# A hybrid trunk in fp32: merge products spread behind their copies, cross-attention K and V between them, output projection in two halves, convolution taps loaded instead of built

## The chip, the cores and the metric

One core of a Trainium2 chip runs the whole kernel in one launch. The core has five engines that run their own instruction queues in order: TensorE (PE, with PEld for its weight loads), VectorE (DVE), ScalarE (ACT), GpSimd (POOL) and SyncE (SP), which here issues nearly all DMA transfers. The metric is the device time of one execution in microseconds (us), lower being better.

## The reference

Two layers over 512 positions of width 1024, all in fp32. Layer 0 mixes tokens with a gated DeltaNet, layer 1 with a Conformer convolution module; after the mixer each layer cross-attends into a fixed memory of 256 rows and applies a squared-ReLU MLP.

```python
def step(state, inp):                      # per chunk of 64 positions, per head
    qd, kd, uc, wc, ai, gl = inp
    v_new = uc - einsum("bhck,bhkv->bhcv", wc, state)
    o = einsum("bhck,bhkv->bhcv", qd, state) + einsum("bhcj,bhjv->bhcv", ai, v_new)
    state = state * exp(gl)[..., None, None] + einsum("bhck,bhcv->bhkv", kd, v_new)
    return state, o
# uc, wc: solution of (I + lower) sol = [v*beta, k*beta*exp(g)], a triangular solve per chunk

def conformer_conv(h, ...):
    u = h @ w_pw1 + b_pw1
    u = u[..., :D] * sigmoid(u[..., D:])
    c = causal_depthwise_conv(u, w_dw) + b_dw          # width 31, per channel
    c = silu(layer_norm(c, ln_g, ln_b))
    return c @ w_pw2 + b_pw2

for layer in range(2):
    h = h + mixer(rms_norm(h))                          # DeltaNet ends in  o @ w_out
    h = h + memory_cross_attention(rms_norm(h), rms_norm(mem), w_q, w_kv, w_o)
    h = h + square(relu(rms_norm(h) @ w_up)) @ w_down
return rms_norm(h, final_norm)
```

## The kernel before

Activations are kept transposed, as eight tiles of 128 channels by 512 positions. An fp32 product is made of three matmuls on values that are split into a high and a low part (`mm3`): high by high, high by low, low by high. Weights come in halves of 128x1024 (512 KB, tile `raw`, three buffers), each loaded by SP, cast to its high part by ScalarE (`wh`, L214) and subtracted by VectorE to give its low part (`wl`, L72). Three split halves may stand ready (`NW`, `NRAW`).

The DeltaNet section is written as a list of units of TensorE work (`mains`). Units 0 to 65 are the projections of k, q, z and v, for head group 0 (heads 0 to 3) and then for group 1: a head's projection is two units of 12 matmuls, so are the z units. Units 66 to 81 are K and V of the first cross-attention, which need only the memory. Beside the units, side work is put at (unit, rank) by `S.at`, and `run` (L275) emits a unit and then its side work by rank. The tile framework turns this into one fixed queue per engine when the kernel is built, with an order that its own planning may change slightly; on the chip each engine works through its queue in order.

The side work that matters here, for each group of four heads:

- `conv_head` (L441 on): the short convolution. For a V head all three further taps are made as a ScalarE scaling (`cvq`, L452) and a POOL add (`cva`, L72); a SiLU on ScalarE (L459) follows a unit later.
- `fs_steps`: a forward substitution on VectorE that inverts 32x32 diagonal blocks (tiles `fst` and `X`), in the units from 20 and from 50 (`FS`). `fs_end` transposes the result (`TB`, `UB`).
- `mg_a` copies the inverse into place for a head: four copies to `x0` on ScalarE (L570), four to `u0` on POOL (L571). It stands at unit 32 (group 0) and 61 to 63 (group 1), `MG`.
- `mg_w`, `mg_y`, `mg_y`, `mg_end`: the merge of the blocks, matmuls of width 96 and less (L579, L591), with a ScalarE copy (`w`, L581; `y`, L594) after each. They stand one to four units behind `mg_a`.
- `v2` transposes V (`vt`, L616), `rec` is the recurrence over four chunks in three steps each, from unit 39 and unit 68 (`REC`), and `o_gate`, `o_norm`, `head_out` finish the heads.

The memory is loaded at unit 53 (`MEM`), squared (`msq`, ScalarE and POOL adds), summed by matmul (`mssq`, L752), scaled by POOL (`mem`, L72) and multiplied by its gain (`mh`, L774). `mem_gain` stands at units 62 and 63, `MGAIN` before the K units. After `run` the output projection w_out is made with all eight heads per output tile (`proj` on `os_`, L1247 on), and `do_ev` adds the residual x, which is loaded again by SP at unit 74.

In the conformer the first three of eight channel blocks are convolved by VectorE (`ca`, L75), paced by `taps_dve`, the other five by TensorE, with a position-phased layout (`xg`, sixteen small DMAs per block, L1014) and nine tap matrices of 128x512 per block. POOL builds the tap matrices from the parameters and an identity (`taps`, L971). In this stretch K of the second cross-attention is computed too.

A line of the changed kernel is two to four lower than the same line here.

Of the kernel before, what the change touches and what calls it, by code (L numbers as in the profile page):

```python
# [9 lines left out]
F32R = mybir.dt.float32r  # L10
# [4 lines left out]
P = 128  # L15
NT = 512
NDVE = 3
# [9 lines left out]
_o += 16  # L27
OFF["w_conv"] = _o
_o += 24 * 4
OFF["w_dw"] = _o  # L30
_o += 8 * 144
OFF["w_tap"] = _o
_o += NDVE * 31
OFF["out_norm"] = _o
# [3 lines left out]


@with_exitstack  # L40
def tile_trunk(ctx, tc, xT, memT, prm_d, adt_d, bdw_d, fin_d, w_ab, w_kq, w_v, w_z, w_dno, w_pw1, w_pw2,
               w_q, w_k, w_vv, w_o, w_up, w_dn, yT):
    nc = tc.nc
    pe, act, dve, pool = nc.tensor, nc.scalar, nc.vector, nc.gpsimd
# [17 lines left out]
    def psum(s="ps"):  # L62
        return psp.tile([P, NT], F32, tag="ps", name=nm(s))
# [4 lines left out]
    def const(shape, s, dt=F32):  # L68
        return cp.tile(list(shape), dt, tag=s, name=s)

    def tt(e, o, a, b, op):
        e.tensor_tensor(out=o, in0=a, in1=b, op=op)  # L72
# [16 lines left out]
    def over_c(t, n=4):  # L89
        return t.unsqueeze(1).to_broadcast([P, n, t.shape[1]])  # L90
# [6 lines left out]
    def load_x():  # L97
        r = []
        for t in range(KT):
            h = slot(s="x")  # L100
            nc.sync.dma_start(out=h, in_=xT[t * P:(t + 1) * P, :])
            r.append(h)
        return r

    nc.sync.dma_start(out=prm[:, 0:NVEC], in_=prm_d[:, 0:NVEC])
    wab = const([P, P], "wab")
    nc.sync.dma_start(out=wab, in_=w_ab)
    raw0 = wp.tile([P, 1024], F32, tag="raw", name="raw0", bufs=NRAW)
    nc.sync.dma_start(out=raw0, in_=w_kq[0][:, 0:1024])
# [26 lines left out]
    headx = const([P, 32], "headx")  # L136
    dve.tensor_reduce(out=headx, in_=ident.rearrange("p (x c) -> p x c", c=4), op=ALU.add, axis=AX.X)
    dve.tensor_reduce(out=headm, in_=headx.rearrange("p (a h) -> p h a", h=8), op=ALU.add, axis=AX.X)
    ident4 = const([P, 32], "ident4")
    eps_rms = const([P, 1], "eps_rms")  # L140
    pool.memset(eps_rms, EPS)
    eps_ln = const([P, 1], "eps_ln")
# [75 lines left out]
    def wnext(key, hf):  # L218
        i = ws["next"]
        assert order[i] == (key, hf), (order[i], key, hf)  # L220
        while ws["load"] < min(i + NRAW + 2, len(order)):
            wload()
        while ws["split"] < min(i + (NW if i else 1), len(order)):
            wsplit()
        ws["next"] += 1
        return ws["hl"].pop(i)
# [11 lines left out]
    def proj(w, xs, ps, k0=0, k1=KT):  # L238
        for k in range(k0, k1):
            mm3(ps, wk(w, k), xs[k], k == 0, k == KT - 1)  # L240
# [729 lines left out]

    def taps(m):  # L971

        w = OFF["w_dw"] + 144 * m
        TAPS[m] = []
        for i in range(9):
            t = slot(s="tap")
            tt(pool, t.rearrange("p (a c) -> p a c", c=32), over_c(ident4, 16),
               prm[:, w + 16 * i:w + 16 * i + 16].unsqueeze(2).to_broadcast([P, 16, 32]), ALU.mult)
            TAPS[m].append(t)

    def conformer(norm, hres, nxt):
# [143 lines left out]

    nc.sync.dma_start(out=prm[:, NVEC:NPRM], in_=prm_d[:, NVEC:NPRM])
    nc.sync.dma_start(out=adt, in_=adt_d.partition_broadcast(P))
    for b in range(4):
        bs = slice(32 * b, 32 * b + 32)
        pool.tensor_copy(ident4[bs, :], ident[bs, bs])  # L1130
    abp = const([P, 2 * P], "abp", F32R)
    ab3 = abp.rearrange("p (k x) -> p k x", k=KT)
    act.copy(ab3[:, :, 0:16], wab.rearrange("p (k x) -> p k x", k=KT))
    tt(dve, ab3[:, :, 16:32], wab.rearrange("p (k x) -> p k x", k=KT), ab3[:, :, 0:16].bitcast(F32), ALU.subtract)
# [68 lines left out]
    for gq in range(2):  # L1203
        f0, nf = FS[gq]
        S.at(f0, 5, D.fs_begin, gq)
        for i in range(nf):
            S.at(f0 + i, 6, D.fs_steps, gq, i * 31 // nf, (i + 1) * 31 // nf)
        S.at(f0 + nf, 0, D.fs_end, gq)
        S.at(f0 + 1, 7, D.norm_k, gq)
        for i in range(4):  # L1210
            h = 4 * gq + i
            m = MG[gq] + i * MSTEP[gq] // 2
            S.at(m, 1, D.mg_a, h)
            S.at(f0 + nf - 4 + i, 5, D.mg_pre, h)
            for j, f in enumerate((D.mg_w, D.mg_y, D.mg_y, D.mg_end)):
                S.at(m + 1 + j, 1, f, h)
        for c in range(4):
            S.at(max(at["v", 4 * gq + 3] + V2[gq], f0 + nf), 3, D.v2, gq, c)
        n = 0
        for c in range(4):  # L1220
            for step in range(3):
                S.at(REC[gq] + n, 0, D.rec, gq, c, step)
                n += 1
            S.at(REC[gq] + n, 5, D.o_gate, gq, c)
        S.at(REC[gq] + n + 1, 1, D.o_norm, gq)
# [3 lines left out]
    S.at(MEM + 9, 3, mem_stat)  # L1229
    S.at(at["kv"] - MGAIN, 6, mem_gain, 0, 0)  # L1230
    S.at(at["kv"] - MGAIN + 1, 6, mem_gain, 0, 1)
    os_, xres = [], []
    for i in range(4):
        S.at(HO + i, 6, lambda i=i: os_.append(D.head_out(i)))
    S.at(REC[1] + 6, 8, lambda: xres.extend(load_x()))
    run(mains, S)

    h = []
# [2 lines left out]
    def do_ev(m, ps):  # L1241
        hn = slot(s="h")
        tt(dve, hn, ps, xres[m], ALU.add)
        h.append(hn)
        n1.add(m, hn)

    def do_w(m):  # L1247
        return wnext(("do", m // 2), m % 2), psum("do")

    w0, p0 = do_w(0)  # L1250
    proj(w0, os_, p0, 0, 4)
    w1, p1 = do_w(1)
    proj(w1, os_, p1, 0, 4)
    for i in range(4, 8):
        os_.append(D.head_out(i))
    proj(w0, os_, p0, 4, 8)
    do_ev(0, p0)
    proj(w1, os_, p1, 4, 8)
    do_ev(1, p1)
    for m in range(2, 8):  # L1260
        w, ps = do_w(m)
        proj(w, os_, ps)
        do_ev(m, ps)
    n2 = Norm("mlp_norm0")
    h = xattn(0, n1, h, n2)
    n3 = Norm("cv_norm", deng=pool)
# [50 lines left out]
    mlp(1, n5, h, None, None, finish, load)  # L1317


NSLOT = 66  # L1320
NCV = 6
NRAW = 3
PRE = ((2, 4), (2, 6))
# [11 lines left out]
FS = ((20, 9), (50, 8))  # L1335
MSTEP = (0, -1)
MG = (32, 63)
V2 = (4, 3)
MGAIN = 4
HO = 76  # L1340
REC = (39, 68)
MEM = 53
MLP_ORDER = [("up", 0), ("up", 1), ("dn", 0), ("up", 2), ("dn", 1), ("up", 3), ("dn", 2), ("dn", 3)]
TAP_RATE = 0.75
CONV_SEQ = [("p", i) for i in range(16)] + [("k", i) for i in range(16)]
# [11 lines left out]
def _pack_a(np, w, order=None):  # L1357
    t = _tiles_a(np, w)
    if order is not None:
        t = t[order]  # L1360
    m = t.shape[0]
    return np.ascontiguousarray(t.reshape(m // 2, 2, 128, 1024).transpose(0, 2, 1, 3).reshape(m // 2, 128, 2048))
# [7 lines left out]

def _taps(np, w):

    wt = w.T.reshape(8, 4, 32, 31)
    e = np.zeros((4, 32, 8, 4, 9, 4), w.dtype)
    for s in range(4):
        for u in range(9):
            for r in range(4):
                d = r - s + 4 * u
                if 0 <= d <= 30:
                    e[s, :, :, :, u, r] = wt[:, :, :, 30 - d].transpose(2, 0, 1)  # L1380
    e = e.reshape(128, 8, 4, 9, 4)
    return np.concatenate([e[:, :, :, 0:8].reshape(128, 8, 128), e[:, :, :, 8].reshape(128, 8, 16)],
                          axis=2).reshape(128, 1152)


def _layout(np, i):
    i = {k: np.asarray(v) for k, v in i.items()}
    f = np.ascontiguousarray

    def vec(v):  # L1390
        return v.reshape(-1, 128).T

    r = {}
    r["xT"] = f(i["x"][0].T)
    r["memT"] = f(i["mem"][0].T.reshape(4, 2, 128, 256).transpose(0, 2, 1, 3).reshape(4, 128, 512))
    vecs = [i["dn_norm"][0], i["cv_norm"][0], i["xa_norm"][0], i["xa_norm"][1], i["xa_mem_norm"][0],
            i["xa_mem_norm"][1], i["mlp_norm"][0], i["mlp_norm"][1], i["cv_ln_g"][0],
            i["cv_ln_b"][0], i["cv_b_pw2"][0], i["cv_b_pw1"][0]]
    cols = [vec(v) for v in vecs]
    cols.append(i["dn_w_conv"][0].T.reshape(24, 128, 4).transpose(1, 0, 2).reshape(128, 96))  # L1400
    cols.append(_taps(np, i["cv_w_dw"][0]))
    cols.append(i["cv_w_dw"][0].T.reshape(8, 128, 31)[:NDVE].transpose(1, 0, 2).reshape(128, NDVE * 31))
    cols.append(i["dn_out_norm"][0].reshape(128, 1))
    r["prm"] = f(np.concatenate(cols, axis=1))
    r["adt"] = f(np.concatenate([i["dn_a_log"][0], i["dn_dt_bias"][0]]))
    r["bdw"] = f(i["cv_b_dw"][0])
    r["fin"] = f(i["final_norm"])
    w = i["dn_w_in"][0]
    r["w_ab"] = f(w[:, 4096:].reshape(8, 128, 16).transpose(1, 0, 2).reshape(128, 128))
    r["w_kq"] = _pack_a(np, w[:, :2048], [8, 9, 10, 11, 0, 1, 2, 3, 12, 13, 14, 15, 4, 5, 6, 7])  # L1410
    r["w_v"] = _pack_a(np, w[:, 2048:3072])
    r["w_z"] = _pack_b(np, w[:, 3072:4096])
    r["w_dno"] = _pack_a(np, i["dn_w_out"][0])
    r["w_pw1"] = _pack_a(np, i["cv_w_pw1"][0], [m for h in range(8) for m in (h, 8 + h)])
    r["w_pw2"] = _pack_a(np, i["cv_w_pw2"][0])
    r["w_q"] = np.stack([_pack_a(np, i["xa_w_q"][j]) for j in range(2)])
    r["w_k"] = np.stack([_pack_a(np, i["xa_w_kv"][j][:, :1024]) for j in range(2)])
    r["w_vv"] = np.stack([_pack_b(np, i["xa_w_kv"][j][:, 1024:]) for j in range(2)])
    r["w_o"] = np.stack([_pack_a(np, i["xa_w_o"][j]) for j in range(2)])
    r["w_up"] = np.stack([_pack_a(np, i["mlp_w_up"][j]) for j in range(2)])  # L1420
    r["w_dn"] = np.stack([np.concatenate([(_pack_b if (j, g) == (1, 3) else _pack_a)(
        np, i["mlp_w_down"][j][g * 1024:(g + 1) * 1024]) for g in range(4)]) for j in range(2)])
    return r
# [17 lines left out]
```

## Time and profile before

| | |
|---|---|
| median of 3 runs | 1583.6 us (1582.46 to 1584.26) |
| the profiled execution, own time | 1584.79 us |
| its span in the profile | 1583.1 us |
| mean granted TensorE clock | 0.984 |
| busy: TensorE, VectorE, ScalarE, POOL | 1539.9, 897.3, 652.5, 239.5 us |
| DMA | 147.57 MB, 28.4% of 16 engines' time on SP's queue |

The page of a profile gives busy time per engine, the span in 40 slices, the DMA queues, the chain of work that ended last, the costliest groups of instructions and the DMA issues. A group's row reads: line, engine, operation, output<-inputs, shape, count, then busy us, mean ns of one, and the engine's idle time just before them with the releaser. A waits row reads: engine, what waited, what it waited for, then us in total, times, longest us. "PEclk" is the clock that TensorE was granted, as a share of full speed.

### The profile page before, as it was taken

What the parts mean: (1) busy time and instruction counts of PE and PEld (TensorE: products, weight loads), DVE (VectorE), ACT (ScalarE), POOL (GpSimd) and SP (SyncE); (2) the same over time, 40 slices, a digit from 0 to 9 for tenths busy, and PEclk for the clock granted to TensorE, in tenths of its full rate; (3) what the DMA queues carried; (4) which work ended last, traced back from release to release, by engine and by line L of the source; (5) the groups of instructions that cost most, each with busy time, mean ns of one, the idle gap of its engine ahead of it and who ended that gap; (6) DMA issues with size and microseconds to landing.
All of it is one profiled execution on the core that took longest, in us unless ns stands there. A gap on an engine that the chain in (4) does not pass through costs nothing.

```text
span 1583.1 us, 19556 instructions
## 1 busy us (share of the span) xinstructions
PE 1539.9 (97%) x7690; PEld 1300.1 (82%) x7690; DVE 897.3 (57%) x1290; ACT 652.5 (41%) x997; POOL 239.5 (15%) x287
## 2 busy tenths in 40 slices
PE   8997997999999999999999999999999999999998
PEld 6886885898888888888888889888888888888886
DVE  6785787576555444343445599974545443443441
ACT  6655574645444433231424321164434432322332
POOL 1225224402111100000021316102012000000000
PEclk9998998799999999999999999999999999999999
DMA  5221112153211233223223422253212232223231
GB/s 180 67 80 54 59 49 94 54 173 119 91 61 64 93 98 102 94 94 101 98 94 95 146 79 92 77 164 103 80 41 94 93 104 96 94 96 104 94 107 53
DMA packets 46699, 147.57 MB, mean 93 GB/s; under 512 B 6288, under 2 KB 8976, under 8 KB 46608
## 3 DMA queue, kind: packets, MB, share of 16 engines
q1 hardware_dynamic: 46608, 146.33, 28.4%
q8 instruction: 60, 0.98, 0.3%
q14 instruction: 31, 0.25, 0.0%
HBM read 142.90 MB, written 2.10 MB: 92 GB/s over the span
## 4 chain that ended last, share of the span: by engine, by line
PE 79%; DVE 11%; ACT 4%; issue 2%; POOL 2%; SPq 1%; DMA 1%; DVEq 0%; POOLq 0%; ACTq 0%
PE up L230 7%; PE up L232 7%; PE up L231 7%; PE dn L232 6%; PE dn L231 6%; PE dn L230 6%; DVE ca L75 3%; PE q L230 2%; PE xo L231 2%; DVE wl L72 2%; PE q L231 2%; PE q L232 2%; PE xo L232 2%; PE xo L230 2%; PE pw L230 2%
## 5 line engine op out<-in xcount | busy, mean ns | idle before, releaser
L214 ACT CAST wh<-raw 128x1024 fp32r<-128x1024 f32 x248 | 260.2, 1051 | 699.6 <-PE dn L231 190.4
L72 DVE TENSOR_TENSOR wl<-raw,wh 128x1024 fp32r<-128x1024 f32 x248 | 310.3, 1252 | 128.6 <-ACT wh L214 122.5
L230 PE MATMUL up<-xh,wh 128*128 128x512 f32 x512 | 200.2, 391 | 0.0
L232 PE MATMUL up<-xh,wl 128*128 128x512 f32 x512 | 199.2, 389 | 0.0
L231 PE MATMUL up<-xl,wh 128*128 128x512 f32 x512 | 199.2, 389 | 0.0
L232 PE MATMUL dn<-uh,wl 128*128 128x512 f32 x448 | 174.3, 389 | 0.0
L230 PE MATMUL dn<-uh,wh 128*128 128x512 f32 x448 | 174.3, 389 | 0.0
L231 PE MATMUL dn<-ul,wh 128*128 128x512 f32 x448 | 174.3, 389 | 0.0
L72 DVE TENSOR_TENSOR h<-dn,h 128x512 f32<-128x512 f32 x56 | 41.8, 747 | 165.3 <-PE dn L232 165.3
L75 DVE SCALAR_TENSOR_TENSOR rl<-up,rb 128x512 f32<-128x512 f32 x64 | 44.2, 691 | 157.0 <-PE up L232 157.0
L231 PEld LDWEIGHTS up<-xl,wh 128*128 128x128 f32 x512 | 96.1, 188 | 20.4 <-issue 0.5
L230 PEld LDWEIGHTS up<-xh,wh 128*128 128x128 f32 x512 | 96.1, 188 | 20.2 <-issue 0.5
L232 PEld LDWEIGHTS up<-xh,wl 128*128 128x128 f32 x512 | 96.1, 188 | 20.0
L72 POOL TENSOR_TENSOR tap<-ident,prm 128x512 f32<-128x512 f32 x45 | 59.4, 1351 | 332.5 <-PE up L232 263.8
L231 PEld LDWEIGHTS dn<-ul,wh 128*128 128x128 f32 x448 | 84.1, 188 | 17.5
L230 PEld LDWEIGHTS dn<-uh,wh 128*128 128x128 f32 x448 | 84.1, 188 | 17.5
L232 PEld LDWEIGHTS dn<-uh,wl 128*128 128x128 f32 x448 | 84.1, 188 | 17.4
L72 POOL TENSOR_TENSOR sq<-sq,sq 128x512 f32<-128x512 f32 x30 | 49.9, 1663 | 252.7 <-ACT sq L305 167.8
L75 DVE SCALAR_TENSOR_TENSOR ca<-x,prm,ca 128x512 f32<-128x512 f32 x90 | 81.9, 911 | 2.1
L230 PE MATMUL h<-xh,wh 128*128 128x512 f32 x192 | 77.0, 401 | 1.4 <-ACT xh L298 1.4
L231 PE MATMUL h<-xl,wh 128*128 128x512 f32 x192 | 76.3, 397 | 1.5 <-DVE xl L75 1.5
L232 PE MATMUL h<-xh,wl 128*128 128x512 f32 x192 | 75.3, 392 | 0.0
(330 smaller groups left out, 3074.9 us busy)
## 6 DMA issues: line engine op xcount, KB each, us to landing
raw<-w_up SPq DMA_DIRECT2D x64, 512.0 KB, 3.4
raw<-w_dn SPq DMA_DIRECT2D x64, 512.0 KB, 3.5
raw<-w_pw SPq DMA_DIRECT2D x24, 512.0 KB, 3.6
raw<-w_kq SPq DMA_DIRECT2D x16, 512.0 KB, 3.6
raw<-w_k SPq DMA_DIRECT2D x16, 512.0 KB, 3.6
raw<-w_vv SPq DMA_DIRECT2D x16, 512.0 KB, 3.7
raw<-w_q SPq DMA_DIRECT2D x16, 512.0 KB, 3.4
raw<-w_o SPq DMA_DIRECT2D x16, 512.0 KB, 3.5
```

Source lines behind the costliest of these rows:

```text
L72: e.tensor_tensor(out=o, in0=a, in1=b, op=op)
L75: dve.scalar_tensor_tensor(out=o, in0=a, scalar=s, in1=b, op0=op0, op1=op1)
L214: act.copy(h, raw)
L230: pe.matmul(ps, wh, xh, start=first, stop=False)
L231: pe.matmul(ps, wh, xl, start=False, stop=False)
L232: pe.matmul(ps, wl, xh, start=False, stop=last)
```

## The change

1. The merge steps of a head stand further behind its copies (`MGLAG`): three units and more in group 0 (with half a unit more per head), six in group 1. `v2` stands seven units behind the last V head in both groups, the recurrence starts at units 42 and 73, the memory is loaded at unit 50, and its gain is applied at units 60 and 61. With this, K units of the first cross-attention come between the copies and the merge of group 1.
2. The output projection is made in two halves: heads 0 to 3 in eight new units 82 to 89, added into the residual tiles; heads 4 to 7 after `run`. The weights are repacked so that a loaded half holds four heads for two output tiles; the residual is loaded at unit 78.
3. The tap matrices are laid out on the host's side of the input arrays and loaded, 45 DMAs of 256 KB on SP; the POOL products, their parameters (w_dw) and the helper identity go.
4. Two small tiles (`wab`, `abp`) use the general slots, of which there are 69 in place of 66.

```diff
-    wab = const([P, P], "wab")
+    wab = slot(s="wab")[:, 0:P]
...
     def taps(m):
-        w = OFF["w_dw"] + 144 * m
         TAPS[m] = []
         for i in range(9):
             t = slot(s="tap")
-            tt(pool, t.rearrange("p (a c) -> p a c", c=32), over_c(ident4, 16),
-               prm[:, w + 16 * i:w + 16 * i + 16].unsqueeze(2).to_broadcast([P, 16, 32]), ALU.mult)
+            nc.sync.dma_start(out=t, in_=tap_d[m - NDVE, i])
             TAPS[m].append(t)
...
-    for b in range(4):
-        bs = slice(32 * b, 32 * b + 32)
-        pool.tensor_copy(ident4[bs, :], ident[bs, bs])
-    abp = const([P, 2 * P], "abp", F32R)
+    abp = slot(F32R, "abp")[:, 0:2 * P]
...
             for j, f in enumerate((D.mg_w, D.mg_y, D.mg_y, D.mg_end)):
-                S.at(m + 1 + j, 1, f, h)
+                S.at(m + MGLAG[gq] + j + (i // 2 if gq == 0 else 0), 1, f, h)
         for c in range(4):
-            S.at(max(at["v", 4 * gq + 3] + V2[gq], f0 + nf), 3, D.v2, gq, c)
+            S.at(at["v", 4 * gq + 3] + V2[gq], 3, D.v2, gq, c)
...
-    os_, xres = [], []
+    os_, xres, wdo = [], [], {}
+    def do_mm(q, m):
+        if m % 2 == 0:
+            wdo[0] = wnext(("do", 2 * q + m // 4), m // 2 % 2)
+        ps = psum("do")
+        for k in range(4):
+            mm3(ps, wk(wdo[0], m % 2 * 4 + k), os_[4 * q + k], k == 0, k == 3)
+        return ps
+    def do_first(m):
+        ps = do_mm(0, m)
+        tt(dve, xres[m], ps, xres[m], ALU.add)
+    at["do"] = len(mains)
+    for m in range(8):
+        mains.append(lambda m=m: do_first(m))
     for i in range(4):
         S.at(HO + i, 6, lambda i=i: os_.append(D.head_out(i)))
-    S.at(REC[1] + 6, 8, lambda: xres.extend(load_x()))
+    S.at(at["do"] - 4, 8, lambda: xres.extend(load_x()))
     run(mains, S)
...
-    w0, p0 = do_w(0)
-    proj(w0, os_, p0, 0, 4)
-    w1, p1 = do_w(1)
-    proj(w1, os_, p1, 0, 4)
     for i in range(4, 8):
         os_.append(D.head_out(i))
-    proj(w0, os_, p0, 4, 8)
-    do_ev(0, p0)
-    proj(w1, os_, p1, 4, 8)
-    do_ev(1, p1)
-    for m in range(2, 8):
-        w, ps = do_w(m)
-        proj(w, os_, ps)
-        do_ev(m, ps)
+    for m in range(8):
+        do_ev(m, do_mm(1, m))
...
-NSLOT = 66
+NSLOT = 69
...
-V2 = (4, 3)
-MGAIN = 4
+MGLAG = (3, 6)
+V2 = (7, 7)
+MGAIN = 6
 HO = 76
-REC = (39, 68)
-MEM = 53
+REC = (42, 73)
+MEM = 50
```

More of the change, by code (lines that the diff above doesn't have):

```diff
@@ L29 @@
 _o += 24 * 4
-OFF["w_dw"] = _o
-_o += 8 * 144
 OFF["w_tap"] = _o
@@ L40, in tile_trunk @@
 @with_exitstack
-def tile_trunk(ctx, tc, xT, memT, prm_d, adt_d, bdw_d, fin_d, w_ab, w_kq, w_v, w_z, w_dno, w_pw1, w_pw2,
+def tile_trunk(ctx, tc, xT, memT, prm_d, adt_d, bdw_d, tap_d, fin_d, w_ab, w_kq, w_v, w_z, w_dno, w_pw1, w_pw2,
                w_q, w_k, w_vv, w_o, w_up, w_dn, yT):
@@ L138, in tile_trunk @@
     dve.tensor_reduce(out=headm, in_=headx.rearrange("p (a h) -> p h a", h=8), op=ALU.add, axis=AX.X)
-    ident4 = const([P, 32], "ident4")
     eps_rms = const([P, 1], "eps_rms")
@@ L1245, in do_ev @@
         n1.add(m, hn)
-    def do_w(m):
-        return wnext(("do", m // 2), m % 2), psum("do")
-    w0, p0 = do_w(0)
-    proj(w0, os_, p0, 0, 4)
-    w1, p1 = do_w(1)
-    proj(w1, os_, p1, 0, 4)
     for i in range(4, 8):
         os_.append(D.head_out(i))
-    proj(w0, os_, p0, 4, 8)
-    do_ev(0, p0)
-    proj(w1, os_, p1, 4, 8)
-    do_ev(1, p1)
-    for m in range(2, 8):
-        w, ps = do_w(m)
-        proj(w, os_, ps)
-        do_ev(m, ps)
+    for m in range(8):
+        do_ev(m, do_mm(1, m))
     n2 = Norm("mlp_norm0")
@@ L1381, in _taps @@
     e = e.reshape(128, 8, 4, 9, 4)
-    return np.concatenate([e[:, :, :, 0:8].reshape(128, 8, 128), e[:, :, :, 8].reshape(128, 8, 16)],
-                          axis=2).reshape(128, 1152)
+    e = np.concatenate([e[:, :, :, 0:8].reshape(128, 8, 128), e[:, :, :, 8].reshape(128, 8, 16)], axis=2)
+    e = e.reshape(4, 32, 8, 9, 16)[:, :, NDVE:]
+    t = np.zeros((8 - NDVE, 9, 4, 32, 16, 32), w.dtype)
+    for c in range(32):
+        t[:, :, :, c, :, c] = e[:, c].transpose(1, 2, 0, 3)
+    return t.reshape(8 - NDVE, 9, 128, 512)
 def _layout(np, i):
@@ L1400, in _layout @@
     cols.append(i["dn_w_conv"][0].T.reshape(24, 128, 4).transpose(1, 0, 2).reshape(128, 96))
-    cols.append(_taps(np, i["cv_w_dw"][0]))
     cols.append(i["cv_w_dw"][0].T.reshape(8, 128, 31)[:NDVE].transpose(1, 0, 2).reshape(128, NDVE * 31))
@@ L1406, in _layout @@
     r["bdw"] = f(i["cv_b_dw"][0])
+    r["tap"] = f(_taps(np, i["cv_w_dw"][0]))
     r["fin"] = f(i["final_norm"])
@@ L1412, in _layout @@
     r["w_z"] = _pack_b(np, w[:, 3072:4096])
-    r["w_dno"] = _pack_a(np, i["dn_w_out"][0])
+    r["w_dno"] = f(_tiles_a(np, i["dn_w_out"][0]).reshape(2, 2, 2, 128, 2, 4, 128).transpose(4, 0, 3, 1, 2, 5, 6)
+                   .reshape(4, 128, 2048))
     r["w_pw1"] = _pack_a(np, i["cv_w_pw1"][0], [m for h in range(8) for m in (h, 8 + h)])
```

## The prediction

> **What bounds the kernel now.** I read the page first, for the share of TensorE, then TensorE's waits, then the table by stretch around each wait, then the chain of waits inside the two longest.
>
> ```profile
> span 1583.1 us, 19556 instructions
> PE 1539.9 (97%) x7690; PEld 1300.1 (82%) x7690; DVE 897.3 (57%) x1290; ACT 652.5 (41%) x997; POOL 239.5 (15%) x287
> ...
> PE mg L579 <- POOL msq L72: 11.2, 1, 11.2
> PE mg L579 <- ACT x L570: 6.8, 2, 6.5
> PE K L232 <- DVE wl L72: 3.7, 1, 3.7
> PE mg L591 <- POOL xg L1009: 3.3, 1, 3.3
> PE mg L591 <- ACT w L581: 2.6, 1, 2.6
> ...
> PE ai L499 <- ACT cva L459: 1.5, 1, 1.5
> PE V L262 <- DVE wl L72: 1.5, 1, 1.5
> ```
>
> TensorE is busy for 97% of the span, so only its idle time and its slow clock can be saved. The page puts 1583.1 us in the span; the profiled execution's own time is 1584.8, 1.2 above the median of 1583.6, and all differences below are added to the median. The waits with "mg" are the merge products. With the 6.5 and the 2.6 the first merge (group 0) idles 9.1 us; with 11.2, 0.3 and 3.3 the second (group 1) idles 14.9. (The page names POOL memsets for 3.3; the real releaser is in the chain below.) The second cost is the clock, in the column after POOL of the table by stretch (columns: stretch, length, then busy time and count of PE, PEld, DVE, ACT, POOL, then PEclk, DMA share, GB/s):
>
> ```profile
> 126.00:136.30 10.30, 5.86 (x28) 5.89 (x28) 4.64 (x6) 9.06 (x21) 5.54 (x13) 0.50 0.16 51
> 139.80:142.40 2.60, 0.05 (x1) 0.08 (x1) 0.00 (x0) 1.20 (x3) 2.52 (x6) 1.00 0.00 0
> 143.20:146.50 3.30, 3.30 (x23) 3.30 (x22) 0.00 (x0) 3.30 (x6) 1.80 (x3) 0.50 0.00 0
> 266.00:283.10 17.10, 8.74 (x37) 7.87 (x38) 3.08 (x4) 10.78 (x21) 13.91 (x25) 0.50 0.06 23
> 293.30:303.60 10.30, 8.45 (x53) 8.12 (x54) 7.61 (x13) 7.11 (x15) 4.88 (x6) 0.50 0.33 102
> 1010.00:1014.00 4.00, 4.00 (x22) 4.00 (x23) 3.93 (x6) 0.00 (x0) 0.00 (x0) 0.57 0.12 31
> ```
>
> Half the busy time at clock 0.50 is lost: 5.86/2 + 3.30/2 = 4.6 us behind the first merge, 8.74/2 + 8.45/2 = 8.6 behind the second, 1.7 behind the wait at 1006. So merge 1 costs 13.7, merge 2 23.5, and the two waits in the conformer 3.7 + 1.7 + 1.5 = 6.9. All four together, 44 us, are the most that this change can gain.
>
> On the second row a rule differs from the trace. The Trainium skill, "TensorE: Matmul & The Clock Gate" (What's actually happening), has the clock fall after at least one idle window of about 3.4 us; here 2.6 us of idleness was followed by 3.3 us at 0.50, so the trace does not bear out a full idle window as the condition. By that page of the Trainium skill a pause of 2 to 3 us would cost no clock, and the tails of such pauses, 1.7 us each, would drop out of the sum below. I go by the trace.
>
> **Merge products, group 0 (MGLAG 3, V2 from 4 to 7).** The first merge matmul needs the 16 x copies on ScalarE and 16 u copies on POOL, which begin when VectorE has transposed the inverse. The chain of waits before:
>
> ```profile
> 135.81 0.38 POOL u L571
> ...
> 138.07 1.28 POOL cva L72
> 139.42 0.41 POOL u L571
> 139.90 1.27 POOL cva L72
> ...
> 141.73 0.48 ACT w L581
> ...
> 147.14 0.23 PE h L231
> 147.37 0.23 PE h L232
> ```
>
> The merge's own ACT copy (w) stands behind a SiLU, and that behind POOL's convolution adds (cva), which share POOL's queue with the u copies. In the built order of the changed kernel that is still so: w of the first head is behind the SiLU of the second V head, whose three adds come after all 16 u copies and the three adds of the head before. POOL is done with the copies about 141.2 (before, 139.8), and with three more adds of 1.27 at 145.3; SiLU and copy give 145.9, the first mg_y 146.5. The filler is real: two V units (12 matmuls at the 0.227 of the last two rows = 2.72 us each) fill 124.0, where the idling began, to 129.45, and one more ends about 137.4, partly at half clock. From there TensorE idles 9 us, where before it idled 6.5 and 2.6 in two pieces. Idle about 10.5 plus tails of 4.5, against 13.7: +1.5. Ends: -13.7 if w comes free before the filler is used up, +4 if both tails are whole. The 1.5 us wait of ai on a SiLU lies at units that V2 and REC shift; I take it as gone, which cancels the +1.5. **Sum: 0.**
>
> **Merge products, group 1, and K in the gap (MGLAG 6, V2 7, REC 73, MGAIN 6).** The before chain and ScalarE's groups in 263 to 300:
>
> ```profile
> 268.06 0.39 POOL u L571
> 268.50 0.39 POOL u L571
> ...
> 284.42 1.30 POOL mem L72
> ```
>
> ```profile
> L570 ACT COPY x<-TB 32x128 f32<-32x128 f32 x16 | 6.5, 408 | 2.0 <-DVE TB L550 1.8
> L452 ACT ACTIVATE cvq<-cv,prm 128x512 f32<-128x512 f32 x8 | 5.3, 709 | 1.8 <-DVE X L72 1.8
> L774 ACT ACTIVATE mh<-mem,prm 128x256 fp32r<-128x256 f32 x8 | 3.5, 499 | 0.5 <-POOL mem L72 0.3
> L214 ACT CAST wh<-raw 128x1024 fp32r<-128x1024 f32 x2 | 2.1, 1039 | 0.0
> L459 ACT ACT_TABLE_LOAD x1 | 1.3, 1283 | 0.0
> ```
>
> Before, the merges stood in TensorE's queue ahead of V's last units; now K stands there. But K's first weight cast (wh, L214) is, in the built order, behind mh, the memory's gain, and behind the SiLU of the seventh V head. Both wait for POOL. POOL's order is 13 u copies from 268.06 at 0.42 (to 273.5), one add 1.27, four mem products (1.3 to 1.4 each, to 280.0), add, copy, add (to 283.0). ScalarE: table load and SiLU to 284.9, three cvq to 286.8, four mh to 288.5, cast to 289.5. TensorE has V's units until about 274.9, including a wait of 3 us for the memory's square sums (mssq now directly after unit 59, its last add on POOL late); MEM moves the memory's four loads, four squares and three POOL adds three units up, the same work earlier. That wait sits in the shadow of the later one and costs nothing, unless K comes early. Idle 274.9 to 289.5 = 14.6, as long as before.
>
> K runs at 24 matmuls a unit with half the columns: 2.9 us, or 5.1 at half clock. First unit to 294.6. The next cast stands behind seven x copies (2.9), a SiLU (0.6), four x copies (1.7) and four convolution scalings (2.5): 298.2. The one behind it waits for three POOL adds, a SiLU and four scalings again: 304.5; the fourth 308.4. TensorE idles some 3 us ahead of each of the first two. From 308.4 five K units (14.4), what is left of the merges (about 5: the first products are 6.7 at half clock in the row below, 3.3 at full, the later ones about as much, and a quarter is done by then) and the V transposes vt (2.0) end at 329.8; I put 330.3 for a last half-clock stretch.
>
> ```profile
> L579 PE MATMUL mg<-x,bt 128*128 128x96 f32 x32 | 6.7, 389 | 11.5 <-POOL msq L72 11.2 <-ACT x L570 0.3
> ...
> 332.30 1.06 PE L674 MATMUL S<-vnd,kt 128*128 128x128 f32 x8
> ```
>
> Before, K's eighth unit ended at 332.3 with 41 recurrence matmuls (0.89 per eight, 4.5) already inside: 327.8 for the same work. **Sum: +2.5.** Ends: -20, if the casts get ahead and only the last tail stays; +8, if the second and third casts come one POOL round later.
>
> **Output projection in two halves.** The 96 x 2 matmuls stay. The first halves (units 82 to 89) use weights from repacked w_dno, the same eight loads of 512 KB. Eight adds from PSUM into xres are new on VectorE; the nearest row is h<-dn,h, 747 ns each, 6 us, in 332 to 489, where VectorE is busy 87.6 of 156.7 us and TensorE never waits:
>
> ```profile
> 332.30:489.00 156.70, 156.68 (x819) 133.63 (x818) 87.59 (x126) 70.68 (x127) 24.48 (x18) 1.00 0.31 101
> L72 DVE TENSOR_TENSOR h<-dn,h 128x512 f32<-128x512 f32 x56 | 41.8, 747 | 165.3 <-PE dn L232 165.3
> ```
>
> The x loads move from unit 74 to 78 on SP and wait there for slots, with the w_dno loads behind them; three raw buffers are then loaded, 8 us of cover. Without it a load (3.5 us) shows. Second halves are 2.72 us per eviction, against about 2.6 of VectorE. Taken +0.5, ends -1 and +4.
>
> **Taps by DMA.** 45 POOL products (59.4 us) become 45 loads of 256 KB, 11.8 MB, on SP's queue. TensorE never waited on POOL's taps; the gain is on VectorE, which is full in 900 to 1040 and slower while POOL works. First row: that stretch; next two: 940 to 1000, with POOL building taps; last two: 1010 to 1100, without.
>
> ```profile
> 900.00:1040.00 140.00, 134.79 (x870) 122.53 (x869) 135.76 (x212) 34.50 (x41) 37.73 (x27) 0.99 0.27 84
> ...
> L75 DVE SCALAR_TENSOR_TENSOR ca<-x,prm,ca 128x512 f32<-128x512 f32 x59 | 58.0, 983 | 1.6
> L72 DVE TENSOR_TENSOR wl<-raw,wh 128x1024 fp32r<-128x1024 f32 x14 | 18.6, 1334 | 0.5 <-ACT wh L214 0.5
> ...
> L72 DVE TENSOR_TENSOR wl<-raw,wh 128x1024 fp32r<-128x1024 f32 x22 | 26.7, 1219 | 7.2 <-ACT wh L214 6.7
> L75 DVE SCALAR_TENSOR_TENSOR ca<-x,prm,ca 128x512 f32<-128x512 f32 x13 | 9.7, 748 | 0.3
> ```
>
> 59 x (983 - 748) + 14 x (1334 - 1219) = 15.5 us of VectorE, ahead of waits of 3.7 and 1.5 on its wl. Both vanish, with the clock tail: -6.9. Against it stands SP's queue, where taps, weight halves and the glu shuffles now alternate:
>
> ```profile
> cy<-bdw SPq DMA_DIRECT2D x8, 256.0 KB, 5.6
> ```
>
> A 256 KB load lands after 5.6 us in a batch of eight. Placing each load in SP's built order behind those that the trace shows there, I estimate the taps of channel blocks 5 and 6 ready 4 and 2 us ahead of their products; a slip beyond that is TensorE's. I take -6.4, ends -6.9 and +4. The first load's 44 and 679 KB parameters shrink by 576 KB behind work that does not wait, four POOL copies go, two constants become slots (66 to 69): 0.
>
> **Sum.** 0 + 2.5 + 0.5 - 6.4 = -3.4: 1580.2 us, with a range of its own of 1574 to 1586.
>
> **Rivals.** (a) *The merges are really filled.* If ScalarE reaches w and K's casts early, merge 1 loses its second half (-7) and merge 2 its idle time but not its tails (-12): with the conformer -25, 1558; in full -44, 1540. For it: the filler exists, 2.72 us a unit, and nothing in TensorE's order forbids it. Against: both chains above pass through POOL, whose copies cannot start before the inverse at 267. (b) *ScalarE starves K.* Each SiLU behind three adds costs K's next cast 3.9 us more if its adds start late; with three such casts, all merges pushed behind them: merge 2 ends +10 instead of +2.5, and the sum is +4, 1588. It decides from a second cast later than 303. For it: adds, copies and mem share POOL. (c) *SP is late in the conformer.* Taps ahead of weight halves: TensorE stops on raw or on taps two or three times, 2 to 4 us each with tails, in place of -6.4 +5: 1591.6. Point of decision: a tap set over 4 us later than I place it. For it: the taps add 11.8 MB to one queue in 130 us. Against: the DMA share there was 0.27. (d) *It does nothing*: VectorE remains full because the ca products fill what is freed, and the wl wait moves; 1586.
>
> **Chances.** Forecast 0.45, (a) 0.24, (b) 0.16, (c) 0.11, (d) 0.04. Differences within 0.2% (3.2 us) are what a measurement here can't tell from none. The forecast's range puts 0.24 faster, 0.16 same, 0.05 slower; with (a) faster, (b) and (c) mostly slower: 0.48, 0.20, 0.32. Range 1558 to 1592.
>
> **What would show it.** Right: TensorE waits behind ACT (w; wh of K) of about 9 and 14 us with tails at 0.50; no wait above 1 us at K and V of the second cross-attention; ca at about 750 ns throughout; no wait on raw or tap. Wrong: no idle piece above 4 us in 124 to 150 or 263 to 305, or new waits on DMA between 930 and 1025.

## The result, and the profile after

The changed kernel takes 1594.4 us (median; 1593.4 to 1599.8) where the kernel before takes 1583.5: 1.0075 times as long, 95% interval 1.0064 to 1.0086; by the medians it is 10.9 us slower. The profiled execution took 1595.0 us with a span of 1593.3, against 1584.8 and 1583.1 before. The prediction was 1580, faster, with a range up to 1592.

First the page of the changed kernel and TensorE's waits (what waited, what it waited for; us in total, times, longest).

```profile
span 1593.3 us, 19541 instructions
PE 1537.4 (96%) x7690; PEld 1295.8 (81%) x7690; DVE 889.7 (56%) x1298; ACT 653.2 (41%) x997; POOL 179.3 (11%) x238
...
PE K L227 <- ACT wh L211: 16.2, 3, 12.6
PE mg L588 <- ACT w L578: 12.7, 1, 12.7
PE mssq L749 <- POOL msq L70: 4.5, 1, 4.5
PE ssq L313 <- DVE sq L70: 2.3, 1, 2.3
PE K L229 <- DVE wl L70: 2.3, 2, 1.1
PE h L228 <- DVE xl L73: 2.0, 1, 2.0
PE ai L496 <- ACT cva L456: 2.0, 1, 2.0
...
PE o L688 <- DVE vn L70: 1.0, 1, 1.0
```

The two long waits of the merge products are still there, one each, under other names: the first merge now waits 12.7 us for ScalarE's copy w, and K waits 12.6 us for its first weight cast where the merge waited 11.2 for POOL. The waits of K and V on wl in the conformer (3.7 and 1.5 before) are gone; the two waits on wl that are left belong to K in the DeltaNet section.

To see where each microsecond went I took every matmul's step from its start to the next start, subtracted the step of the same tile at full speed, and summed the rest by stretches that hold the same work in all kernels. This counts idle time and slow clock together. All runs of the study but e12 stand in it; the stretches are named by what TensorE does there. Each row is one profiled execution. The four kernels with the merges and the adds of before (before, e2, e4, e8) spread from 15.2 to 16.7 in merge 1 and from 24.0 to 26.3 in group 1 and K, so differences of that size show nothing.

```
us lost              start  merge 1  ai, o  group 1 and K  output  conformer  (rest)
before                12.0    16.7    2.3       26.3         0.9      8.7      7.3
after                 15.4    20.1    3.9       32.6         1.5      2.9      8.0
e1 parameters back    12.8    20.9    4.2       32.6         1.5      3.2      7.6
e2 taps alone         12.3    15.8    2.3       24.0         0.9      2.4      7.2
e3 part 1 alone       12.5    19.7    4.2       32.5         5.5      9.0      7.4
e4 halves alone       12.0    15.2    2.2       25.5         1.0      8.6      7.4
e5 SiLU late          12.8    12.0    5.8       29.4         1.5      2.3      7.6
e6 + mem on VectorE   12.6    12.1    5.8       25.1         1.5      3.6      7.4
e7 e5 + adds on VecE  12.4    11.4    5.9       24.3         1.5      2.4      7.5
e8 part 1 undone      12.4    15.8    2.3       25.6         1.0      2.2      7.5
e9 e7 + mem on VecE   12.7    11.5    4.2       19.3         1.5      2.4      7.4
e10 + memory early    12.8    11.5    4.3       17.3         1.5      2.2      7.3
e11 e8 + adds         12.6    13.3    2.2       20.9         1.0      2.2      7.5
```

Between before and after the sums differ by 10.2 us, which is what the spans differ by. Start +3.4, merge 1 +3.4, ai and o +1.6, group 1 and K +6.3, output +0.6, conformer -5.8, rest +0.7. So the change gains 5.8 us in the conformer and loses more than twice as much, 15.3 us, in the DeltaNet section with the start ahead of it.

The first merge on the changed kernel, ScalarE and then POOL (start, duration, engine, instruction, count, in brackets the idle time before and its releaser):

```profile
133.06 6.86 ACT L567 COPY x<-TB 32x128 f32<-32x128 f32 x16 [0.41 <-DVE TB L547]
142.04 0.63 ACT L456 ACTIVATE cva<-cva 128x512 f32<-128x512 f32 x1 [2.12 <-POOL cva L70]
...
145.03 1.03 ACT L211 CAST wh<-raw 128x1024 fp32r<-128x1024 f32 x1
151.63 0.63 ACT L456 ACTIVATE cva<-cva 128x512 f32<-128x512 f32 x1 [5.57 <-POOL cva L70]
152.16 0.85 ACT L578 ACTIVATE w<-mg 128x384 f32<-128x384 f32 x2
```

```profile
142.07 3.03 POOL L568 COPY u<-UB 32x128 f32<-32x128 f32 x7
...
145.20 0.95 POOL L519 MEMSET DB<- 128x1024 f32 x1
146.08 0.95 POOL L527 MEMSET X<- 128x1024 f32 x1
...
147.32 4.27 POOL L70 TENSOR_TENSOR cva<-cva,cvq 128x512 f32<-128x512 f32 x3
```

ScalarE has nothing to do for 5.6 us, with w ready to be made, because a SiLU that nobody needs yet stands ahead of it and waits for POOL. For K it is the same queue, with the memory's gain (mh) ahead of the cast as well:

```profile
285.30 0.91 ACT L771 ACTIVATE mh<-mem,prm 128x256 fp32r<-128x256 f32 x2 [4.92 <-POOL mem L70]
286.52 0.91 ACT L771 ACTIVATE mh<-mem,prm 128x256 fp32r<-128x256 f32 x2 [0.32 <-POOL mem L70]
...
292.13 0.63 ACT L456 ACTIVATE cva<-cva 128x512 f32<-128x512 f32 x1 [2.80 <-POOL cva L70]
...
296.10 1.03 ACT L211 CAST wh<-raw 128x1024 fp32r<-128x1024 f32 x1
```

### The profile page after: what moved, and what is told of

Same layout as the page of the kernel before. It is cut to its first block, busy times and chain, and to the rows that moved or that the text cites. A ratio compares the mean times of both kernels' runs of the same rounds, so it can differ in the third digit from the quotient of the medians.

```text
span 1593.3 us, 19541 instructions
## 1 busy us (share of the span) xinstructions
PE 1537.4 (96%) x7690; PEld 1295.8 (81%) x7690; DVE 889.7 (56%) x1298; ACT 653.2 (41%) x997; POOL 179.3 (11%) x238
## 4 chain that ended last, share of the span: by engine, by line
PE 84%; DVE 7%; ACT 4%; POOL 2%; issue 1%; DMA 1%; SPq 0%; POOLq 0%; DVEq 0%; ACTq 0%
PE up L228 7%; PE up L227 7%; PE up L229 7%; PE dn L228 6%; PE dn L227 6%; PE dn L229 6%; PE pw L227 3%; PE pw L229 3%; PE pw L228 3%; PE q L227 2%; PE xo L228 2%; PE q L229 2%; PE q L228 2%; PE xo L227 2%; PE xo L229 2%; DVE wl L70 2%
## 5 line engine op out<-in xcount | busy, mean ns | idle before, releaser
L70 DVE TENSOR_TENSOR wl<-raw,wh 128x1024 fp32r<-128x1024 f32 x248 | 306.6, 1237 | 148.9 <-ACT wh L211 137.7
L229 PEld LDWEIGHTS up<-xh,wl 128*128 128x128 f32 x512 | 96.1, 188 | 19.9
L73 DVE SCALAR_TENSOR_TENSOR ca<-x,prm,ca 128x512 f32<-128x512 f32 x90 | 67.2, 748 | 1.6
L227 PE MATMUL K<-mh,wh 128*128 128x256 f32 x128 | 38.5, 301 | 16.2 <-ACT wh L211 16.2
```

What stands on the lines that cost most here:

```text
L73: dve.scalar_tensor_tensor(out=o, in0=a, scalar=s, in1=b, op0=op0, op1=op1)
L227: pe.matmul(ps, wh, xh, start=first, stop=False)
L229: pe.matmul(ps, wl, xh, start=False, stop=last)
```

## The experiments

The theory: in-order queues of ScalarE and POOL hold w and K's casts, so that the filler placed in the gap cannot run (theory 1), and the taps' gain is independent of it. The rivals stand with each run; where an expectation says theory 1, it is this one applied to that run (in e1 it is the parameter load). Ratios are to the kernel before, run beside each group of experiments, with medians of 1583.3 to 1584.8 us. e1 to e4 and e8 take the parts of the change apart, e5 to e7, e9 and e10 test the mechanism, e11 and e12 ask whether the move of the merges is worth anything.

**e1: the smaller parameter load.** What differs at the start is the load of the parameters (679 KB, now 103), two constants in slots, and the number of slots. e1 puts the load back, and the 66 slots with it to make room.

```diff
+OFF["w_dw"] = _o
+_o += 8 * 144
...
+    cols.append(np.zeros((128, 1152), np.float32))
...
-NSLOT = 69
+NSLOT = 66
```

> The changed kernel with the 1152 unread tap parameters put back into the second parameter load (679 KB again; 66 slots to make room). Theory 1: the smaller load made the planner put two weight casts ahead of the squares on ScalarE, and the kernel lost 3.4 us before 60 us; with the load back the casts stand behind the squares, the losses before 60 us are 9.4 us again in place of 12.8, and the time is 1591. Rival: the delay comes from wab and abp in slots, which stay here: 1594.4 and 12.8.

Measured 1593.1 us, ratio 1.0059 (1.0040 to 1.0078) against 1.0075 for the changed kernel; the two intervals overlap, so the time alone does not decide. The start does: its loss falls from 15.4 to 12.8 us, near the 12.0 of before. ScalarE's order at the start of the changed kernel and of e1:

```profile
7.64 4.39 ACT L295 ACTIVATE xh<-x,prm 128x512 fp32r<-128x512 f32 x7
13.38 1.04 ACT L211 CAST wh<-raw 128x1024 fp32r<-128x1024 f32 x1 [1.34 <-DMA raw<-w_kq]
14.33 0.72 ACT L295 ACTIVATE xh<-x,prm 128x512 fp32r<-128x512 f32 x1
15.32 1.05 ACT L211 CAST wh<-raw 128x1024 fp32r<-128x1024 f32 x1 [0.28 <-DMA raw<-w_kq]
16.27 4.28 ACT L302 ACTIVATE sq<-x 128x512 f32<-128x512 f32 x8
```

```profile
8.11 5.00 ACT L297 ACTIVATE xh<-x,prm 128x512 fp32r<-128x512 f32 x8
13.02 4.25 ACT L304 ACTIVATE sq<-x 128x512 f32<-128x512 f32 x8
17.18 1.98 ACT L213 CAST wh<-raw 128x1024 fp32r<-128x1024 f32 x2
```

With the smaller load the built order has two casts ahead of the squares. On the chip the casts wait for their DMA, the squares come 3 us later, and the sum of squares (ssq) on TensorE waits 2.3 us, with a half-clock stretch behind it; in e1 that wait is gone. No run separates the load from the number of slots. Built with 66 slots and the small load, the kernel still has both casts ahead of the squares, which points to the load; why the planner orders them so is not shown. The remaining 0.8 us of the start is not explained; the other kernels with the large load lie between 12.0 and 12.8.

**e2: taps by DMA alone**, in the kernel before, with the old parameters kept.

```diff
-            tt(pool, t.rearrange("p (a c) -> p a c", c=32), over_c(ident4, 16),
-               prm[:, w + 16 * i:w + 16 * i + 16].unsqueeze(2).to_broadcast([P, 16, 32]), ALU.mult)
+            nc.sync.dma_start(out=t, in_=tap_d[m - NDVE, i])
```

> The kernel before with taps by DMA alone; the parameters stay in their load. Theory 1: the waits of 3.7 and 1.5 us in the conformer and the clock tail vanish: -5.9, 1577.6. Rival: the conformer gained only because everything ran 16 us later behind the same transfers, or the 45 loads delay weight halves when nothing is late: 1581 to 1586.

Measured 1577.3 us, ratio 0.9956 (0.9940 to 0.9972): theory 1. The conformer loses 2.4 us in place of 8.7. VectorE's convolution steps in 940 to 1000, in the kernel before (first row) and in e2:

```profile
L75 DVE SCALAR_TENSOR_TENSOR ca<-x,prm,ca 128x512 f32<-128x512 f32 x41 | 44.5, 1087 | 1.2
...
L75 DVE SCALAR_TENSOR_TENSOR ca<-x,prm,ca 128x512 f32<-128x512 f32 x37 | 27.7, 748 | 0.9
L72 DVE TENSOR_TENSOR wl<-raw,wh 128x1024 fp32r<-128x1024 f32 x7 | 8.5, 1218 | 6.1 <-ACT wh L214 6.1
```

They take 748 ns, as predicted, and no wait on raw or tap appears. In this stretch they took 1087 before; the prediction's 983 is the mean over 940 to 1040.

**e3: part 1 alone** (merge lag, v2, recurrence, memory, gain).

```diff
-                S.at(m + 1 + j, 1, f, h)
+                S.at(m + MGLAG[gq] + j + (i // 2 if gq == 0 else 0), 1, f, h)
...
-V2 = (4, 3)
-MGAIN = 4
-REC = (39, 68)
-MEM = 53
+MGLAG = (3, 6)
+V2 = (7, 7)
+MGAIN = 6
+REC = (42, 73)
+MEM = 50
```

> The kernel before with the moves of part 1 alone (MGLAG, V2, REC, MEM, MGAIN). Theory 1: the merges' waits move behind ScalarE and POOL and grow: merge 1 +2.6 to +3.5, squares of the memory and K +6.3, ai and o +1.5: +10 to +12, 1594 to 1596, with waits of mg on w and of K on wh of over 10 us each. Rival: the two stalls are so long only because the start was late and the inverse with it (275.6 against 267): without that +0 to +4, 1584 to 1588.

Measured 1602.3 us, ratio 1.0116 (1.0099 to 1.0133), 18.4 us slower by the ratio: more than theory 1 said, and far from the rival, so a late start is not the cause. Merge 1 (+3.0), ai and o (+1.9) and group 1 with K (+6.2) came as in the changed kernel. Of the rest, 4.6 us is in the output stretch: the recurrence, five units later, now runs where no units are left beside it, and TensorE waits in it five times for 0.4 to 0.9 us. In the changed kernel the eight new units cover it (1.5).

**e4: output projection in halves alone** (the functions `do_mm` and `do_first` and the repacked weights put into the kernel before, all else as before).

> The kernel before with the output projection in two halves alone. Theory 1: hidden, 0 to +1, 1583.5 to 1584.5, and no wait of TensorE between 335 and 415 us. Rival: the later loads of x and the eight added evictions show: +3 or more, 1586.5.

Measured 1583.7 us, ratio 0.9999 (0.9990 to 1.0009): no difference, as theory 1 said. By e3 and the changed kernel the halves are worth those 4 us only once the recurrence is later; no run has these two parts without the others.

**e5: SiLU of V later**, on e1.

```diff
-LAG = (0, 0, 1)
+LAG = (0, 0, 5)
```

> e1 with the SiLU of each V head four units later (LAG 5 in place of 1), so that it stands behind neither w nor K's first casts; POOL's work is the same. Theory 1 (ScalarE's queue order holds both): the wait of mg on w falls from 12.3 to under 4 us, K's first cast comes some 5 us earlier and the next two 6 to 8, so merge 1 loses 9 less and the gap of group 1 7 less: about 1577. Rival (POOL's u copies and mem products are what both wait for in the end): 0 to -4, 1589 to 1593.

Measured 1582.0 us, ratio 0.9990 (0.9980 to 0.9999), 11 us better than e1: between the two, nearer to theory 1. Merge 1 loses 12.0 us in place of 20.9, the 9 that were expected, and its wait on w is 4.4 us, where under 4 was expected. So the SiLU in ScalarE's queue was the cause there. ai and o lose 1.6 us more than in e1. Group 1 gains only 3.2 of the expected 7, and its longest wait (first row) stays:

```profile
PE K L229 <- ACT wh L213: 13.0, 3, 11.9
...
PE mg L590 <- ACT w L580: 4.4, 1, 4.4
```

K's cast was no longer behind a SiLU but was still behind mh. ScalarE idled 4.9 us for POOL's mem products ahead of the first two mh, and 2.1 us for one of POOL's adds ahead of the last four.

**e6: mem products on VectorE**, on e5.

```diff
-            tt(pool, m.rearrange("p (k t) -> p k t", k=2), ...
+            tt(dve, m.rearrange("p (k t) -> p k t", k=2), ...
```

> e5 with the four mem products on VectorE in place of POOL. In the built order K's first cast now stands ahead of mh. Theory 1: K's first cast is done before V's last unit ends, the 12 us wait of K on wh is gone, the gap of group 1 loses 12 to 17 us in place of 32: 1565 to 1570. Rival (K is held by ml and by later casts): at most 5 us better than e5, 1572 or more.

Measured 1578.1 us, ratio 0.9963 (0.9951 to 0.9976), 4 us better than e5: the rival's size. The cast came early, as theory 1 said, but other things of the same two queues took its place:

```profile
PE K L229 <- ACT mh L773: 4.2, 1, 4.2
PE K L229 <- ACT wh L213: 3.4, 1, 3.4
```

**e7: fewer POOL adds**, on e5: two of three further taps of a V head on VectorE.

```diff
-CONV_K, CONV_Q, CONV_V = 0, 1, 3
+CONV_K, CONV_Q, CONV_V = 0, 1, 1
```

> e5 with two of three further convolution taps of each V head on VectorE (CONV_V 1), so POOL has 16 adds fewer and ScalarE 16 scalings fewer; mem products on POOL. Theory 1: POOL's chain is shorter by some 2.5 us a head, K's casts come earlier than in e5 and those behind them too: 1571 to 1575. Rival: VectorE is full before the inverse, the adds delay it by up to 5 us: 1578 to 1583.

Measured 1576.1 us, ratio 0.9955 (0.9940 to 0.9970), 6 us better than e5, 1 us outside theory 1's range. The wait of K on wh is gone; K now waits for ml, which VectorE makes from the mem products:

```profile
PE K L230 <- DVE ml L75: 6.6, 3, 6.0
```

**e8: part 1 undone**, output halves and taps kept, parameters as in e1.

> e1 with part 1 taken back (merge steps, v2, recurrence, memory at their former units): output halves and taps by DMA with the old parameter load. Theory 1: e2 and e4 add up, -6 + 0: 1577.5. Rival: the parts interact (the eight new units and K): 1580 or more.

Measured 1577.8 us, ratio 0.9966 (0.9955 to 0.9978): e2 and e4 add up. Against e1 (1.0059) part 1 costs 0.93%, 14.7 us, in the company of the other parts.

**e9: both.** e7 with the mem products on VectorE.

> e7 with the mem products on VectorE as in e6. Theory 1 (each operation taken off POOL's and ScalarE's path to K counts): the wait of 6.0 us of K on ml halves, 1571 to 1574. Rival: VectorE now holds K (mem, ml and wl in one queue): 1576 or more.

Measured 1570.6 us, ratio 0.9919 (0.9904 to 0.9934): theory 1, slightly better than its range. K's longest wait on ml fell to 2.7 us; a wait of 3.8 on wl came in.

**e10: memory one unit earlier**, on e9.

```diff
-MEM = 50
+MEM = 49
```

> e9 with the memory one unit earlier (MEM 49). Theory 1: the last square is no longer behind a weight cast that waits for TensorE, the wait of mssq on msq (4.5 us, 1.5 of half clock behind it) goes, and K's first cast stands ahead of the x copies: 6 us less than e9, 1566 to 1568. Rival (my prediction's: the mssq wait lies in the shadow of the later wait of K and costs nothing): e9's time within 2 us.

Measured 1568.9 us, ratio 0.9907 (0.9892 to 0.9922). Against e9 that is 1.7 us, not 6: the rival's size, and the two intervals overlap. The wait of mssq went from 4.5 to 2.4 us and no further:

```profile
PE mg L590 <- ACT w L580: 6.8, 3, 4.7
PE K L229 <- ACT mh L773: 3.1, 1, 3.1
PE mssq L751 <- POOL msq L72: 2.4, 1, 2.4
```

It is the fastest kernel of the study by its median, 14.7 us under before by the ratio (0.9907), with everything of the change in it but the smaller parameter load and the three further slots.

**e11: the former merge with fewer adds**, e8 with CONV_V 1.

> e8 (merge steps at their former units) with CONV_V 1 as in e7. If POOL's adds hold the merges there too, merge 1 and the gap of group 1 lose 3 to 5 us less: 1573 to 1575. If not, 1577.8. Against e10 it tells whether the move of the merges is worth anything once its queues are free.

Measured 1571.0 us, ratio 0.9919 (0.9902 to 0.9935), 7 us better than e8, more than expected: merge 1 -2.5, group 1 and K -4.7. POOL's adds held the merges of the former order as well. And e11 and e10 (0.9907) cannot be told apart: with their queues freed, the moved merges are worth at most a few microseconds over the unmoved ones. e10 also has the mem products on VectorE, the later SiLU and the earlier memory; no run gives these to the unmoved merges, so the worth of the move alone stays open.

**e12: only group 0's merge moved**, on e11, with the SiLUs of its four V heads four units later. The edit is shown against the changed kernel.

```diff
-            S.at(u + lag, 4.1, D.silu, d, key)
+            S.at(u + (5 if key in (0, 1, 2, 3) and d is D.VT else lag), 4.1, D.silu, d, key)
...
-MGLAG = (3, 6)
-V2 = (7, 7)
-MGAIN = 6
+MGLAG = (3, 1)
+V2 = (7, 3)
+MGAIN = 4
...
-REC = (42, 73)
-MEM = 50
+REC = (42, 68)
+MEM = 53
```

> e11 with the merge of group 0 alone moved (MGLAG 3, its SiLUs four units later, V2 7, REC 42). From the losses by stretch: merge 1 -4 against e8, the stretch after it +3.6 (o and ai): no more than 1 us from e11 either way. If the o and ai waits come with group 1's moves, 3 to 4 us faster than e11.

Measured 1569.8 us, ratio 0.9917 (0.9897 to 0.9936): no difference from e11, as expected. Its profiled execution took 5 us longer than its three others, so its stretches are not used.

## Why the prediction was wrong

The sign was wrong, and the time fell outside the range. The forecast summed to -3.4, the stretches to +10.2. The 13.6 us between them are group 1 and K (3.8), the start (3.4), ai and o (3.1), merge 1 (1.9), and 1.4 for the rest. The signs that the prediction named for being right all came: TensorE waited 12.7 us behind w and 12.6 behind K's cast, with the clock at 0.50 behind both, ca took 748 ns, and there was no wait on raw or tap. They tested the order of the queues and not the sizes of the terms, nor the start. By its own steps:

- **Conformer: right.** Predicted -6.4, measured -5.8 in the change and -6 alone (e2). ca went to 748 ns from 983 over 940 to 1040 (the prediction's two rows for 940 to 1000 are of this longer stretch; 940 to 1000 alone had 1087), and the loads were not late, with a DMA share of 0.55 in 970 to 1030:

```profile
970.00:1030.00 60.00, 60.00 (x438) 56.21 (x437) 46.31 (x96) 9.88 (x11) 0.00 (x0) 1.00 0.55 190
```

- **Output in halves: right.** Predicted +0.5, measured +0.6, and 0 alone (e4). What the prediction did not see is that without them the later recurrence costs 4 us more (e3).
- **The start: wrong.** The step that failed is the 0 for the parameters that shrink "behind work that does not wait" and the two constants in slots. The order of ScalarE's queue changed, and TensorE waited for the squares: +3.4, of which e1 returned 2.6. The prediction used the built order only from the merges on.
- **Merge 1: the mechanism was right, the size was not.** That w would stand behind a SiLU behind POOL's adds was predicted, and e5 shows it: with the SiLU moved away 9 us come back. Predicted idle 9 us, measured 12.7 (12.3 in e3, which has the start of before). Two terms were short: POOL's queue holds 2 us of memsets (DB, X) between the copies and the three adds, which I left out, and the adds took 4.3 us together, not 3.8 (4.8 in e3). So +3.4 for +1.5.
- **The ai wait: wrong.** I let it vanish (-1.5) because V2 and REC move the units around it. It grew from 1.5 to 2.0, and o got a wait of 1.0. The reason given was no mechanism, only a move, and no run shows why it grew.
- **Group 1 and K: the mechanism was right, the size was not.** The order on POOL and ScalarE and the spacing of the casts came out as worked: behind the first cast the next three ended 8.7, 15.0 and 18.9 us later in the prediction, and 8.7, 15.6 and 19.9 in the trace.

```profile
296.10 1.03 ACT L211 CAST wh<-raw 128x1024 fp32r<-128x1024 f32 x1
304.84 1.03 ACT L211 CAST wh<-raw 128x1024 fp32r<-128x1024 f32 x1
311.66 1.03 ACT L211 CAST wh<-raw 128x1024 fp32r<-128x1024 f32 x1
316.00 1.03 ACT L211 CAST wh<-raw 128x1024 fp32r<-128x1024 f32 x1
```

  From the fourth cast to K's end the prediction had 21.9 us, the trace 26.3 (317.0 to 343.3). The failed term is "what is left of the merges (about 5": the rows of merge matmuls behind the fourth cast hold 8.7 us, of which the later products (with w) alone are 7.1 where the prediction had 3.3, and K's third unit ended 1.8 us behind that cast. With 26.3 for 21.9 the sum is +6.9, measured +6.3.

```profile
L588 PE MATMUL mg<-y,w 96*64 96x64 f32 (+1 forms) x64 | 3.9, 210 | 0.0
L588 PE MATMUL mg<-u,w 128*96 128x96 f32 x32 | 3.2, 248 | 0.0
...
L576 PE MATMUL mg<-x,bt 128*128 128x96 f32 x12 | 1.6, 270 | 0.0
```

- **The wait of mssq in the shadow of K's: not settled.** Where K still waited, 4.5 us of mssq (3 in the prediction) stood ahead of 12.6 of K, as said; no run took it away there. In e10 K still waited 5.7 us in all (7.8 in e9), and 2.1 us less of mssq stood beside a time 1.7 us shorter, which the intervals do not resolve.
- **Rivals (b) and (c) had the sign, but not by their mechanisms.** (b), ScalarE starves K, had 1588, with 0.16. By the letter its sign is met: the second cast ended at 305.9, later than 303. But the first had already ended 7.6 us later than worked (297.1 for 289.5), behind the losses of the start, merge 1, and ai and o, and the second followed at the forecast's 8.7; the further 3.9 us per cast did not come. Group 1 lost 6.3 for another reason, the merges above, where (b) had 10. (c), SP late in the conformer, was nearest in time with 1591.6, by luck: TensorE waited there for no load. What the forecast and the rivals all missed are the start and the wait of ai, each given zero or better in one sentence.
- **The clock rule.** The page of the Trainium skill, "TensorE: Matmul & The Clock Gate" (What's actually happening), has the clock fall after at least one idle window of about 3.4 us. The changed kernel again shows it falling behind less: TensorE idled 2.3 us ahead of ssq (22.6 to 24.9), and the next rows stand at 0.92 and 0.58; in e1, without that wait, the same two stretches stand at 1.00. The measurement decides.

```profile
23.65:27.06 3.41, 2.12 (x12) 1.90 (x13) 1.23 (x2) 0.99 (x1) 0.00 (x0) 0.92 0.43 142
27.06:30.48 3.42, 3.42 (x10) 2.68 (x9) 0.95 (x3) 0.56 (x2) 0.00 (x0) 0.58 0.03 12
```

## What to carry to other kernels

Filler in the bottleneck engine's queue runs only if what it needs is early in the other engines' queues too: before moving work into a gap, read what stands ahead of the filler's inputs on every in-order queue, memsets and activations for later included. Moving the activation that nobody needed yet (one number) was worth 11 us (e5 against e1), where the moved merges showed no gain clear of the intervals in any run (e10 against e11). And where a planner orders the queues, compare the whole built order, from the first instruction: an edit elsewhere can reorder an engine that it does not touch.

## What the runs showed that I had not expected

- A parameter load that shrank by 576 KB went with a slower start, through ScalarE's order: the start's loss was 15.4 us with the small load and 69 slots, and 12.8 with the large one and 66.
- Two parts that do nothing or harm alone can need each other: the halves are worth 0 alone (e4), and with the later recurrence the output stretch loses 5.5 us without them (e3) and 1.5 with them (the changed kernel).
- A POOL add of 128x512 took 1.27 us in most places, and the third of the three ahead of w took 2.1 us in e3:

```profile
144.58 1.27 POOL cva L72
...
145.92 2.13 POOL cva L72
```
